# A macaron layer in split fp32 on one core: keys transposed once, decay columns in two passes, x by half pairs and in scratch during the mixer, weight terms requested ahead

## The chip, the core and the metric

The kernel runs on one core of a Trainium2 chip. The metric is device time in microseconds. Three runs of the kernel before took 1249.96, 1250.2 and 1250.56 us, the median 1250.2. One more execution was profiled; it took 1248.93 us, and its trace spans 1247.2 us. Lines named L.. are lines of the kernel file. TensorE is called PE in the trace, VectorE DVE, ScalarE ACT, GpSimdE POOL, SyncE SP. SP computes nothing here: it issues DMA requests, one behind the other.

## The reference: what is computed

One layer works on 520 tokens: a prompt of 512 and eight single tokens, each with its own states. The model width is 1024, the hidden width of an FFN 2816 = 22 x 128; all values are fp32.

```python
def layer(x, pos, s_ret, s_gdn, s_conv, ...):
    x = x + 0.5 * rmsnorm(swiglu(rmsnorm(x, ffn1_pre_g), ffn1_w_gate, ffn1_w_up, ffn1_w_down), ffn1_post_g)
    m, s_ret_new, s_gdn_new, s_conv_new = token_mixer(rmsnorm(x, mix_pre_g), ...)
    x = x + rmsnorm(m, mix_post_g)
    x = x + 0.5 * rmsnorm(swiglu(rmsnorm(x, ffn2_pre_g), ffn2_w_gate, ffn2_w_up, ffn2_w_down), ffn2_post_g)

def token_mixer(h, ...):
    proj = (h @ w_in).astype(f32)
    rq, rk, rv, rg, conv_in, gz, ga, gb, gate_r, gate_g = jnp.split(proj, idx, axis=-1)
    ...   # retention: 4 heads of 128 with rotary q, k; a short convolution over q, k, v of the gated DeltaNet
    gk = gk * lax.rsqrt(jnp.sum(gk * gk, axis=-1, keepdims=True) + EPS)
    beta = jax.nn.sigmoid(gb)
    g_gdn = -jnp.exp(gdn_a_log.astype(f32)) * jax.nn.softplus(ga + gdn_dt_bias.astype(f32))
    o_g, s_gdn_new = gated_delta_chunked(gq, gk, gv, g_gdn, beta, s_gdn.astype(f32))
    ...
    y = (jax.nn.sigmoid(gate_r) * (o_r @ w_ret_branch) + jax.nn.sigmoid(gate_g) * (o_g @ w_gdn_branch))
    y = (y @ w_out).astype(h.dtype)
```

`ga` and `gb` are four columns each of `w_in`, one for each head. These eight columns are called the decay columns here.

## The kernel before, in words

**Tiles.** x lies transposed: width on 128 partitions in eight tiles, tokens along the row, in two halves of 260. A weight column block is 128x1024 (eight pieces of 128x128, one for each piece k of the width).

**Split fp32.** A weight is split into a rounded part `whi` (a cast on ACT, L301) and a rest `wlo` (a subtraction on DVE, L302); x is split the same way into `xh` and `xl` (`xhl`, L449 on ACT and L450 on DVE). `passes` (L355) does three matmuls of 128x128 by 128x260 for each k: whi with xh (L359), whi with xl (L360), wlo with xh (L361).

**FFNs.** Hidden column pairs (gate and up) are worked on one after the other. The first three pairs of FFN1 and four of FFN2 are plain products, of two raw loads each. All later pairs take seven products instead of eight half-size ones (a Strassen scheme, `product7`, names `sv`), which work on sums of weight quarters and on sums of x quarters (`token_factors`, names ta, tb, th, tl). The weight sums s1 and s3 are made in memory: SP loads one term (L235 and L236), and POOL issues a DMA that adds the other onto it (L258). a22 is the quarter loaded alone (L237). The sums s2 and s4 are made on DVE (L315, L323). `split_seven` (L304) splits one of the seven at a time, on ACT (L319) and DVE (L320). The down projections work in the same way (names `dn`), and `post` (L508) scales by the root of the mean square and adds to x (t L540 on DVE, x L542 on POOL), and splits the new x for the next stage.

**Mixer.** Projections by `w_in` column blocks, then four retention and four DeltaNet heads (`ret_head`, `gdn_head`), the decode tokens' states, the branches and `wo`. The decay columns are the first unit, padded to 128 columns; `gate_rows` scales its rows, `gates` (L1101) transposes them and computes decays on ACT and DVE. `gdn_head` transposes keys and queries by `transposed` (four TensorE transposes of 128x128 into one bank, `tr`, L1093) for their sums of squares (four Squares on ACT, L1304), and later transposes the keys once more, scaled by DVE on the way out of PSUM (L1359, `gkd`).

**Order.** Nothing is scheduled by the compiler: each engine does its instructions in the order in which the program emits them. The program advances by ticks between groups of matmuls. At each tick, `add_sums` (L255) emits the accumulations that are due, `prefetch` (L263) emits splits ahead of use, and spawned coroutines emit their next step. `load_to` (L225) emits the loads two units ahead (RAW_BUFS = 2 raw buffers), a seven pair counting as one unit. So a raw load that waits for its buffer (the reader is `wlo`, or the last sum of a pair) holds up all requests that come behind it on SP. Split weights have nine buffers; `cost` (L260) says how many a unit takes, two for a plain one and one for one of seven. `prefetch` stops where the buffers are spent. Everything larger (x, y, hidden tiles, factors, weight terms) takes one of 68 slots of a shared pool (`slot`, L205), given out in a ring; a tile waits until the slot's last reader is done.

**x.** Loaded at the start in sixteen half-tile requests (L953, L897). During the FFNs' products the x tiles are given up and loaded again in the down projection, in FFN1 from the input, in FFN2 from a copy in DRAM that `keep` stores behind the mixer (L936). During the mixer x stays in eight slots.

## Time and profile before

| what | value |
|---|---|
| three runs: lowest, median, highest | 1249.96, 1250.2, 1250.56 us |
| profiled execution | 1248.93 us |
| its span in the trace | 1247.2 us |
| mean granted TensorE clock | 0.982 |
| busy TensorE, DVE, ACT, POOL | 96%, 72%, 46%, 22% of the span |
| bytes moved by DMA | 166.61 MB, 134 GB/s in the mean |

The stages by the trace: FFN1 to about 366 us, the mixer to about 865, FFN2 from there, of which the last 14 us are the final scaling and the stores. Times in the trace are from the span's start. Rows of instructions give start, duration, engine, line, operation, output and input names, shapes and count; the bracket gives the idle time of that engine ahead of the row and what ended it. A row with x2 or more spans several instructions. Matmuls overlap, so one lasts 0.28 us in the trace and the next begins 0.12 us behind it.

### The profile page before, as it was taken

To read this page: it belongs to the slowest core of one execution; us is meant where nothing else is said; L and a number is where in the kernel's file an instruction comes from. 1 tells how busy PE (TensorE), PEld (TensorE's weight loads), DVE (VectorE), ACT (ScalarE), POOL (GpSimd) and SP (SyncE) were. 2 spreads that over 40 slices of the span, in tenths; PEclk is the share of its full clock that TensorE was granted. 3 is DMA by queue.
4 is the path that set the end of the run, shared out by engine and by line. 5 is a ranking of instruction groups with operands and counts; after the bars stand their busy time and mean duration, and the time that the engine had idled before them with its cause. 6 is when DMAs were issued, how large, how long until landed. Compare 5 with 4: busy or idle time off the path is not lost.

```text
span 1247.2 us, 25546 instructions
## 1 busy us (share of the span) xinstructions
PE 1199.9 (96%) x9953; PEld 1187.0 (95%) x9953; DVE 904.1 (72%) x1941; ACT 570.4 (46%) x1203; POOL 279.5 (22%) x502
## 2 busy tenths in 40 slices
PE   8899999999998999999999999999989999999995
PEld 7899999999998999999999999999989999999995
DVE  8788888776557887768676666547958888866554
ACT  6555666553335564312334333334635656653330
POOL 4111111000014248545441112204111111100003
PEclk8999999999999999999999999999989999999998
DMA  5677777333353233332444554322377777532352
GB/s 178 176 178 180 182 184 184 91 94 94 94 168 90 86 103 98 98 111 71 130 140 122 188 180 154 117 86 84 115 209 178 179 177 183 146 92 66 106 165 69
DMA packets 78538, 166.61 MB, mean 134 GB/s; under 512 B 16977, under 2 KB 21937, under 8 KB 78417
## 3 DMA queue, kind: packets, MB, share of 16 engines
q1 hardware_dynamic: 66128, 140.69, 35.5%
q0 software_dynamic: 12288, 24.29, 11.3%
q8 instruction: 78, 1.28, 0.4%
q14 instruction: 44, 0.35, 0.1%
HBM read 155.24 MB, written 9.70 MB: 132 GB/s over the span
## 4 chain that ended last, share of the span: by engine, by line
PE 66%; DVE 15%; DMA 7%; ACT 6%; issue 3%; POOL 2%; SPq 1%; ACTq 0%; DVEq 0%; POOLq 0%
PE sv L359 9%; PE sv L361 8%; PE sv L360 8%; PE p L359 6%; PE p L360 5%; PE p L361 5%; PE dn L361 5%; PE dn L359 5%; PE dn L360 5%; DMA s<-gu_in 4%; DVE wlo L302 3%; DMA raw<-dn_in 2%; ACT whi L301 1%; PE br L359 1%; PE br L360 1%
## 5 line engine op out<-in xcount | busy, mean ns | idle before, releaser
L359 PE MATMUL p<-xhl,whi 128*128 128x260 f32 x784 | 233.0, 297 | 0.0
L360 PE MATMUL p<-xhl,whi 128*128 128x260 f32 x784 | 223.6, 285 | 0.0
L361 PE MATMUL p<-xhl,wlo 128*128 128x260 f32 x784 | 223.1, 285 | 0.0
L359 PE MATMUL sv<-th,w 128*128 128x260 f32 x592 | 168.2, 284 | 4.5 <-ACT u L771 4.5
L302 DVE TENSOR_TENSOR wlo<-raw,whi 128x1024 fp32r<-128x1024 f32 (+2 forms) x121 | 142.6, 1184 | 40.7 <-ACT whi L301 38.9
L361 PE MATMUL sv<-th,w 128*128 128x260 f32 x592 | 168.0, 284 | 0.0
L360 PE MATMUL sv<-tl,w 128*128 128x260 f32 x592 | 167.9, 284 | 0.0
L359 PEld LDWEIGHTS p<-xhl,whi 128*128 128x128 f32 x784 | 149.7, 191 | 0.7
L360 PEld LDWEIGHTS p<-xhl,whi 128*128 128x128 f32 x784 | 149.9, 191 | 0.1
L361 PEld LDWEIGHTS p<-xhl,wlo 128*128 128x128 f32 x784 | 149.7, 191 | 0.1
L320 DVE TENSOR_TENSOR w<-s,w 128x512 fp32r<-128x512 f32 x148 | 101.4, 688 | 55.2 <-ACT w L319 53.1
L258 POOL DMA_DIRECT2D s<-gu_in x74 | 65.0, 963 | 323.0 <-DMA s<-gu_in 178.2
L359 PE MATMUL sv<-xhl,w 128*128 128x260 f32 x444 | 126.3, 284 | 6.5 <-DVE t L751 5.9
L361 PE MATMUL dn<-hh,wlo 128*128 128x260 f32 x448 | 127.1, 284 | 1.9 <-DVE wlo L302 1.9
L301 ACT CAST whi<-raw 128x1024 fp32r<-128x1024 f32 (+2 forms) x121 | 116.5, 971 | 26.1 <-DMA raw<-dn_in 18.4
L359 PE MATMUL dn<-hh,whi 128*128 128x260 f32 x448 | 127.2, 284 | 0.1
L360 PE MATMUL dn<-hl,whi 128*128 128x260 f32 x448 | 126.6, 283 | 0.0
L361 PE MATMUL sv<-xhl,w 128*128 128x260 f32 x444 | 125.9, 283 | 0.0
L360 PE MATMUL sv<-xhl,w 128*128 128x260 f32 x444 | 125.6, 283 | 0.0
L319 ACT CAST w<-s 128x512 fp32r<-128x512 f32 x148 | 91.4, 619 | 62.8 <-DVE s L315 32.8
L359 PEld LDWEIGHTS sv<-th,w 128*128 128x128 f32 x592 | 112.3, 190 | 5.2 <-ACT u L771 4.9
L360 PEld LDWEIGHTS sv<-tl,w 128*128 128x128 f32 x592 | 112.3, 190 | 0.0
(407 smaller groups left out, 3270.0 us busy)
## 6 DMA issues: line engine op xcount, KB each, us to landing
raw<-gu_in SPq DMA_DIRECT2D x50, 512.0 KB, 4.7
raw<-win_in SPq DMA_DIRECT2D x49, 512.0 KB, 3.6
s<-gu_in SPq DMA_DIRECT2D x74, 256.0 KB, 5.5
s<-gu_in POOLq DMA_DIRECT2D x74, 256.0 KB, 4.5
raw<-dn_in SPq DMA_DIRECT2D x32, 448.0 KB, 3.4
a<-gu_in SPq DMA_DIRECT2D x37, 256.0 KB, 5.8
raw<-dn_in SPq DMA_DIRECT2D x16, 512.0 KB, 3.6
x<-x SPq DMA_DIRECT2D x16, 260.0 KB, 5.4
```

What stands on the lines that cost most here:

```text
L258: self.nc.gpsimd.dma_start(out=out, in_=term, accum_op=ALU.add)
L301: self.nc.scalar.copy(hi[:, ks], t[:, ks])
L302: self.nc.vector.tensor_tensor(lo[:, ks], t[:, ks], hi[:, ks].bitcast(F32), ALU.subtract)
L319: nc.scalar.copy(w[:, 0], t[i])
L320: nc.vector.tensor_tensor(w[:, 1], t[i], w[:, 0].bitcast(F32), ALU.subtract)
L359: mm(ps, hi[:, k, :], xh, start=first, stop=False, skip_group_check=more)
L360: mm(ps, hi[:, k, :], xl, start=False, stop=False, skip_group_check=more)
L361: mm(ps, lo[:, k, :], xh, start=False, stop=last, skip_group_check=more)
```

## The change

Five things are changed.

1. The decay columns come as their own array of eight columns for each k (`wab`, 32 KB instead of 512 KB). Their hi and lo parts lie side by side in one tile of 16 columns, so that two passes (16 columns with xh, 8 with xl) do what three did: 32 matmuls, not 48. `gates` transposes 16 rows and adds the two parts (two copies on ACT, two adds on DVE). The unit counts as one split.
2. In each of the four DeltaNet heads the keys are copied out of PSUM on ACT at the first transposition, and the second transposition is dropped. DVE scales the copy.
3. x lies in tiles of two pieces by one half. The start's sixteen requests of 130 KB become eight of 260 KB; the layouts of input and output follow.
4. x is stored to DRAM behind FFN1 (`keep`, x1) and loaded again in the mixer's down projection (`load_x`), its eight slots are given back in between.
5. The three terms of a seven pair are requested by `begin_pair`, s3 first. For the first two pairs of an FFN `token_factors` calls it at its start; each later pair's terms stand ahead of its own raw load instead of behind it.

```diff
+AB = 2 * H
...
-            out += [("win", i, 0, 8) for i in range(n)]
+            out += [("wab", 0, 0, 8)] + [("win", i, 0, 8) for i in range(1, n)]
...
+                s1, s3, a22 = self.begun.pop((u[1], m), None) or self.begin_pair(u[1], m)
                 t = self.raw.tile([P, KD, P], F32, tag="raw", name=self.name("raw"))
-                s1, s3, a22 = (self.slot(x, (P, KH, P)) for x in ("s1", "s3", "a22"))
                 nc.sync.dma_start(out=t, in_=w[2 * m])
-                nc.sync.dma_start(out=s1, in_=w[2 * m + 1, :, 0:KH])
-                nc.sync.dma_start(out=s3, in_=w[2 * m, :, 0:KH])
-                nc.sync.dma_start(out=a22, in_=w[2 * m + 1, :, KH:KD])
-
-                self.sums_due.append((self.now + SUM_LAG, self.raw_next, s1, w[2 * m + 1, :, KH:KD]))
-                self.sums_due.append((self.now + SUM_LAG, self.raw_next, s3, w[2 * m + 1, :, 0:KH]))
                 t = [t[:, 0:KH], s3, None, a22, t[:, KH:KD], s1, None]
             elif u[0] == "down7":
                 t = []
...
-                t = self.raw.tile([P, k1 - k0, P], F32, tag="raw", name=self.name("raw"))
+                t = self.raw.tile([P, k1 - k0, AB if kind == "wab" else P], F32, tag="raw", name=self.name("raw"))
...
+    def begin_pair(self, f, m):
+
+        dma, w = self.nc.sync.dma_start, self.a[f"gu{f}"]
+        s1, s3, a22 = (self.slot(x, (P, KH, P)) for x in ("s1", "s3", "a22"))
+        dma(out=s3, in_=w[2 * m, :, 0:KH])
+        dma(out=s1, in_=w[2 * m + 1, :, 0:KH])
+        dma(out=a22, in_=w[2 * m + 1, :, KH:KD])
+
+        g = self.group[self.unit_list.index(("seven", f, m, 0))]
+        self.sums_due.append((self.now + SUM_LAG, g, s3, w[2 * m + 1, :, 0:KH]))
+        self.sums_due.append((self.now + SUM_LAG, g, s1, w[2 * m + 1, :, KH:KD]))
+        return s1, s3, a22
 
...
-        return 1 if self.unit_list[j][0] in ("seven", "down7") else 2
+        return 1 if self.unit_list[j][0] in ("seven", "down7", "wab") else 2
...
+        if self.unit_list[j][0] == "wab":
+
+            self.load_to(j)
+            w, t = self.whl.tile([P, KD, 2 * AB], F32R, tag="w", name=self.name("wab")), self.loaded[self.group[j]]
+            self.split_done[j] = (w,)
+            self.started(j)
+            self.nc.scalar.copy(w[:, :, 0:AB], t)
+            self.nc.vector.tensor_tensor(w[:, :, AB:], t, w[:, :, 0:AB].bitcast(F32), ALU.subtract)
+            return
...
+        if len(w) == 1:
+            mm(ps[0 : 2 * AB], w[0][:, k, :], xh, start=first, stop=False)
+            mm(ps[0:AB], w[0][:, k, 0:AB], xl, start=False, stop=last)
+            return
...
+    def x_tiles(self):
+
+        return [[self.slot("x", (P, 2, HC)) for _ in range(KH)] for _ in range(2)]
+
+    def x_of(self, k, hf):
+        return self.x[hf][k // 2][:, k % 2]
+
...
-            self.x = [self.slot("x") for _ in range(KD)]
-            for k in range(KD):
-                nc.sync.dma_start(out=self.x[k], in_=x_from[:, k, :])
+            self.x = self.x_tiles()
+            for hf in range(2):
+                for k in range(0, KD, 2):
+                    nc.sync.dma_start(out=self.x[hf][k // 2], in_=x_from[:, hf, k : k + 2])
...
             yield 0
+
+        for m in range(PLAIN[f], PLAIN[f] + 2):
+            self.begun[f, m] = self.begin_pair(f, m)
...
         self.spawn(begin())
         xs, r = self.ffn(PLAIN[1], xs, r, V_G1PRE, self.gh[:, 0:8], V_MPRE, plus1, None, a["xT"])
-        xs, r = self.mixer(xs, r, plus2)
-        x2 = self.dram.tile([P, KD, TOK], F32, name="x2")
-
-        def keep():
-            while len(xs[1]) < KD or r[1] is None:
-                yield 0
-            for k in range(KD):
-                nc.sync.dma_start(out=x2[:, k, :], in_=self.x[k])
-                yield 1
-
-        self.spawn(keep())
+        x1, x2 = (self.dram.tile([P, 2, KD, HC], F32, name=n) for n in ("x1", "x2"))
+        self.spawn(self.keep(x1, xs, r))
+        xs, r = self.mixer(xs, r, plus2, x1)
+        self.spawn(self.keep(x2, xs, r))
         self.ffn(PLAIN[2], xs, r, V_G2PRE, self.gh[:, 8:16], None, plus2, None, x2)
         self.finish()
+
+    def keep(self, out, xs, r):
+
+        x = self.x
+        while len(xs[1]) < KD or r[1] is None:
+            yield 0
+        for hf in range(2):
+            for k in range(0, KD, 2):
+                self.nc.sync.dma_start(out=out[:, hf, k : k + 2], in_=x[hf][k // 2])
+                yield 1
     def load_first(self):
...
-            for z in (k, k + 1):
-                nc.sync.dma_start(out=self.x[z][:, 0:HC], in_=a["xT"][:, z, 0:HC])
+            nc.sync.dma_start(out=self.x[0][k // 2], in_=a["xT"][:, 0, k : k + 2])
...
         for i in range(NCH):
-            self.tr(pt[:, i * 8 : i * 8 + 8], rows[0:8, i * P : (i + 1) * P])
-        self.tr(pt[0:DEC, 32:40], rows[0:8, SEQ:TOK])
+            self.tr(pt[:, i * 16 : i * 16 + 16], rows[0:16, i * P : (i + 1) * P])
+        self.tr(pt[0:DEC, 64:80], rows[0:16, SEQ:TOK])
+        ab = c.tile([P, 5, AB], F32, name="ab")
+        nc.gpsimd.memset(ab, 0.0)
+        pl = self.small("pl", [P, 5, AB])
+        ptv = pt[:, 0:80].rearrange("p (c g) -> p c g", g=16)
+        for rs, cs in ((slice(0, P), slice(0, NCH)), (slice(0, DEC), slice(NCH, 5))):
+            nc.scalar.copy(pl[rs, cs], ptv[rs, cs, AB:])
+            nc.vector.tensor_tensor(ab[rs, cs], ptv[rs, cs, 0:AB], pl[rs, cs], ALU.add)
         ga = c.tile([P, 5, H], F32, name="ga")
         gb = c.tile([P, 5, H], F32, name="gb")
-        nc.gpsimd.memset(ga, 0.0)
-        nc.gpsimd.memset(gb, 0.0)
-        dt = self.vec[:, V_DT : V_DT + H]
-        ptv = pt[:, 0:40].rearrange("p (c g) -> p c g", g=8)
-        nc.vector.tensor_tensor(ga[:, 0:4, :], ptv[:, 0:4, 0:4], dt.unsqueeze(1).to_broadcast([P, 4, H]), ALU.add)
-        nc.vector.tensor_tensor(ga[0:DEC, 4, :], ptv[0:DEC, 4, 0:4], dt[0:DEC], ALU.add)
-        nc.vector.tensor_copy(gb[:, 0:4, :], ptv[:, 0:4, 4:8])
-        nc.vector.tensor_copy(gb[0:DEC, 4, :], ptv[0:DEC, 4, 4:8])
+        nc.vector.tensor_tensor(ga, ab[:, :, 0:H], self.vec[:, V_DT : V_DT + H].unsqueeze(1).to_broadcast([P, 5, H]), ALU.add)
         yield 8
         t = [self.small(f"sp{i}", [P, 5, H]) for i in range(5)]
...
+        kd = sl("gkd", (P, NCH, P))
         for src, off in ((k, NCH), (q, 0)):
             pt = self.transposed(src)
+            if off:
+                nc.scalar.copy(kd.rearrange("p c i -> p (c i)"), pt)
             for i in range(NCH):
...
-        kd = sl("gkd", (P, NCH, P))
-        pk = self.transposed(k)
-        nc.vector.tensor_tensor(kd, pk.rearrange("p (c i) -> p c i", i=P), self.bc(rkd), ALU.mult)
+        nc.vector.tensor_tensor(kd, kd, self.bc(rkd), ALU.mult)
```

**SP, the first seven pairs of FFN2.** Here `raw` of gu_in are the plain pairs' loads up to L251 (L246 in the change) and a seven pair's own at L234 (L235), `s` and `a` the terms, x the copies to DRAM. Before:

```order
L251 DMA raw_11552<-gu_in 128x1024
L251 DMA raw_11558<-gu_in 128x1024
L251 DMA raw_11800<-gu_in 128x1024
L251 DMA raw_11806<-gu_in 128x1024
L936 DMA x_11496<-x_4736 128x520
...
L936 DMA x_11496<-x_4739 128x520
L234 DMA raw_11918<-gu_in 128x1024
L235 DMA s_1969_11919<-gu_in 128x512
L236 DMA s_1970_11920<-gu_in 128x512
L237 DMA a_1971_11921<-gu_in 128x512
```

And in the change:

```order
L246 DMA raw_11538<-gu_in 128x1024
L246 DMA raw_11544<-gu_in 128x1024
L254 DMA s_1936_11768<-gu_in 128x512
L255 DMA s_1935_11767<-gu_in 128x512
L256 DMA a_1937_11769<-gu_in 128x512
L254 DMA s_1939_11774<-gu_in 128x512
L255 DMA s_1938_11773<-gu_in 128x512
L256 DMA a_1940_11775<-gu_in 128x512
L246 DMA raw_11798<-gu_in 128x1024
...
L975 DMA x_5035<-x_11019 128x520
L235 DMA raw_11920<-gu_in 128x1024
L975 DMA x_5035<-x_11020 128x520
```

Six terms now stand ahead of the last two plain loads; before, the first of them stood behind these, behind stores of x and behind its pair's raw.

**SP, the first seven pairs of FFN1.** Before:

```order
L251 DMA raw_284<-gu_in 128x1024
L234 DMA raw_395<-gu_in 128x1024
L235 DMA s_68_396<-gu_in 128x512
L236 DMA s_69_397<-gu_in 128x512
L237 DMA a_70_398<-gu_in 128x512
L234 DMA raw_524<-gu_in 128x1024
L235 DMA s_101_525<-gu_in 128x512
L236 DMA s_102_526<-gu_in 128x512
```

In the change:

```order
L246 DMA raw_276<-gu_in 128x1024
L254 DMA s_59_361<-gu_in 128x512
L255 DMA s_58_360<-gu_in 128x512
L256 DMA a_60_362<-gu_in 128x512
L254 DMA s_62_367<-gu_in 128x512
L255 DMA s_61_366<-gu_in 128x512
L256 DMA a_63_368<-gu_in 128x512
L235 DMA raw_399<-gu_in 128x1024
L235 DMA raw_524<-gu_in 128x1024
L254 DMA s_128_676<-gu_in 128x512
```

The six terms of two pairs stand ahead of both raws; the third pair's terms follow the second pair's raw.

**DVE, the end of FFN1.** `wlo_4829` belongs to the last down unit, the next split to the decay columns, and `wlo_4974` (`wlo_4845` in the change) to the unit behind them. Before:

```order
L302 TENSOR_TENSOR wlo_4829<-raw_4756,whi_4828 128x1024
L302 TENSOR_TENSOR wlo_4835<-raw_4808,whi_4834 128x1024
L461 TENSOR_TENSOR acc_643_3494<-acc_643_3494,s_4908 128x260
L608 TENSOR_SCALAR y_4907<-dn_4840,gh 128x260
L414 SCALAR_TENSOR_TENSOR ms_4935<-ss_4931,plus_12_135 87x3
L540 TENSOR_TENSOR t_4961<-y_3714,rb_4957 128x260
L540 TENSOR_TENSOR t_4970<-y_4007,rb_4957 128x260
L302 TENSOR_TENSOR wlo_4974<-raw_4832,whi_4973 128x1024
L540 TENSOR_TENSOR t_4993<-y_4063,rb_4957 128x260
```

In the change:

```order
L319 TENSOR_TENSOR wlo_4821<-raw_4748,whi_4820 128x1024
L308 TENSOR_TENSOR wab_4826<-raw_4800,wab_4826 128x8x8
L319 TENSOR_TENSOR wlo_4845<-raw_4824,whi_4844 128x1024
L489 TENSOR_TENSOR acc_643_3486<-acc_643_3486,s_4905 128x260
L636 TENSOR_SCALAR y_4904<-dn_4831,gh 128x260
L435 SCALAR_TENSOR_TENSOR ms_4932<-ss_4928,plus_12_127 87x3
L568 TENSOR_TENSOR t_4958<-y_3706,rb_4954 128x260
L568 TENSOR_TENSOR t_4967<-y_3999,rb_4954 128x260
L568 TENSOR_TENSOR t_4984<-y_4055,rb_4954 128x260
```

The split of the unit behind the decay columns moves from behind the first two `t` of the scaling to ahead of the last `acc`. On ACT its `whi` moves in the same way ahead of `s`, which feeds that `acc`.

More of the change, by code (lines that the diff above doesn't have):

```diff
@@ L270, in prefetch @@
             j = self.split_next
-            seven = self.cost(j) == 1
+            seven = self.unit_list[j][0] in ("seven", "down7")
             if self.unit_list[j][0] == "seven" and self.hold_sums and not force:
@@ L464, in square @@
         c0, n = HALVES[hf]
-        x, out = self.x[k][:, c0 : c0 + n], self.sq[k][:, c0 : c0 + n]
+        x, out = self.x_of(k, hf), self.sq[k][:, c0 : c0 + n]
         if eng is self.nc.scalar:
@@ L666, in first_units @@
                     if hf:
-                        self.release()
+                        self.release(len(ws[j]))
                     else:
-                        banks[j][0] = early[j // 2][:, j % 2 * HC : j % 2 * HC + cols]
-                        self.nc.scalar.copy(banks[j][0], ps[j])
+                        rows = 2 * AB if len(ws[j]) == 1 else P
+                        banks[j][0] = early[j // 2][0:rows, j % 2 * HC : j % 2 * HC + cols]
+                        self.nc.scalar.copy(banks[j][0], ps[j][0:rows])
                 if hf:
@@ L679, in token_factors @@
             yield 0
+        for m in range(PLAIN[f], PLAIN[f] + 2):
+            self.begun[f, m] = self.begin_pair(f, m)
         tt, stt = nc.vector.tensor_tensor, nc.vector.scalar_tensor_tensor
         for k in range(KH):
-            x1, x2 = self.x[k], self.x[k + KH]
-            x11, x12, x21, x22 = x1[:, 0:HC], x1[:, HC:TOK], x2[:, 0:HC], x2[:, HC:TOK]
+            x11, x12, x21, x22 = (self.x_of(z, hf) for z in (k, k + KH) for hf in range(2))
             g1, g2 = (self.vec[:, gcol + z : gcol + z + 1] for z in (k, k + KH))
@@ L885, in run @@
         nc.sync.dma_start(out=self.vec, in_=a["vec"])
-        self.x = [self.slot("x") for _ in range(KD)]
+        self.x = self.x_tiles()
         self.ones = c.tile([P, P], F32, name="ones")
@@ L1759 @@
 OUTS = {
-    "yT": (P, KD, TOK),
+    "yT": (P, 2, KD, HC),
     "sretp": (H, P, P),
```

34 lines of the change are left out of this document (17 added, 17 removed).

## Prediction

> **What bounds the kernel now.** I read the busy time of the engines first, then what TensorE waited for, then the busy time by stretch, and at last the chain of waits up to each place that stood out.
>
> ```profile
> PE 1199.9 (96%) x9953; PEld 1187.0 (95%) x9953; DVE 904.1 (72%) x1941; ACT 570.4 (46%) x1203; POOL 279.5 (22%) x502
> PE sv L359 <- DVE t L751: 5.9, 1, 5.9
> PE sv L359 <- ACT u L771: 4.5, 2, 3.8
> PE sv L359 <- DVE v L788: 0.5, 1, 0.5
> 62.00:240.00 178.00, 178.00 (x1489) 178.00 (x1488) 151.08 (x295) 107.36 (x222) 27.96 (x32) 1.00 0.69 172
> 374.00:400.00 26.00, 22.65 (x187) 21.77 (x187) 21.60 (x42) 16.57 (x38) 12.83 (x16) 1.00 0.25 69
> 432.00:640.00 208.00, 202.04 (x1751) 198.45 (x1751) 154.82 (x439) 77.62 (x182) 113.63 (x284) 0.99 0.35 105
> 912.00:923.00 11.00, 5.05 (x31) 4.88 (x30) 7.94 (x15) 5.48 (x11) 1.74 (x2) 0.69 0.68 165
> ```
>
> The rows of waits give the total, how often, and the longest. The rows of stretches give length, busy PE, PEld, DVE, ACT and POOL, then the granted clock, the DMA share and GB/s. TensorE is busy for 1199.9 of 1247.2 us (9953 matmuls, 0.12 each), so about 47 us can be won without removing a product. Two single waits, 5.9 and 3.8 us, both before `sv` products, hold a fifth of that. From 62 to 240 us the same kind of product runs with nothing idle: a pair in steady flow costs no wait, and only the first pairs of each FFN do.
>
> **Terms requested ahead, FFN1.** This is the chain up to the second seven-product pair, and TensorE and ScalarE there.
>
> ```profile
> 42.67 0.33 SPq L234
> 43.05 3.91 DMA s<-gu_in
> 48.15 7.91 DMA s<-gu_in
> 56.16 1.14 ACT L319 CAST w<-s 128x512 fp32r<-128x512 f32 x2 [5.09 <-DMA s<-gu_in]
> 53.55 0.28 PE L361 MATMUL sv<-th,w 128*128 128x260 f32 x1
> 57.62 0.39 PE L359 MATMUL sv<-th,w 128*128 128x260 f32 x1 [3.80 <-ACT u L771]
> 59.09 0.42 PE L360 MATMUL sv<-tl,w 128*128 128x260 f32 x1
> 61.86 0.42 PE L359 MATMUL sv<-th,w 128*128 128x260 f32 x1
> 62.08 0.33 PE L360 MATMUL sv<-tl,w 128*128 128x260 f32 x1
> ```
>
> The wait is put down to the copy `u`, but ScalarE holds that copy behind casts which stood 5.09 us for a sum. The sum's load left SP only at 43.05, behind a raw load that waited for a raw buffer until 42.67; then come 3.91 us of load and 7.91 us of accumulation. In the change both terms of this pair leave SP before that raw load, behind plain raws, the last of which is issued near 26 us:
>
> ```profile
> 21.22 5.43 SPq L251 DMA_DIRECT2D raw<-gu_in  x2
> 35.81 1.97 POOL L258 DMA_DIRECT2D s<-gu_in  x2 [7.71 <-DMA s<-gu_in]
> ```
>
> Six term DMAs at about 0.47 us each leave by 30; the first pair's accumulations start at 35.81 now, so the second's, behind them on POOL, start by 38 and with the slow 7.91 are in by 46. ScalarE would go on at 56.16 − 5.09 = 51.07, and `u`, which follows the two casts (1.14), at 52.2 instead of 57.3: ahead of 53.55, where TensorE's last matmul before the wait starts. So the **3.80 us** go whole. Behind the wait matmuls follow each other by 0.22 us (61.86 to 62.08) and last 0.42 where 0.28 is usual; from about 58.7 to 62.1 that is 3.4 us at 0.12/0.22 of the pace, some 1.5 us lost. I take 5.3 in all; the bounds are 2 (half of the idle time: the raw load of 42.67, which does not move, or the DVE splits end last instead) and 5.5. What is late next is the third pair: its terms now leave right behind the raw load of 42.67, ten us ahead of before.
>
> ```profile
> 431.36 0.42 PE L360 MATMUL p<-xhl,whi 128*128 128x260 f32 x1
> ```
>
> Whether the slow stretch goes with a wait that is only shortened is open. This row, slow at 431.36, stands a little behind a wait of 1.11 us and some short products (427.78, below), so by the trace a short wait may keep it. [...]
>
> **Terms requested ahead, FFN2.**
>
> ```profile
> 868.04 21.24 SPq L251 DMA_DIRECT2D raw<-gu_in  x4
> 898.91 0.43 SPq L235 DMA_DIRECT2D s<-gu_in  x1
> 905.02 8.29 DMA s<-gu_in
> 884.60 1.65 POOL L416 TENSOR_TENSOR rs<-ms,mhalf 87x6 f32<-87x6 f32 x1 [7.58 <-DVE ms L412]
> 914.03 0.69 DVE L320 TENSOR_TENSOR w<-s,w 128x512 fp32r<-128x512 f32 x1 [8.77 <-ACT w L319]
> 918.48 0.76 DVE L751 TENSOR_TENSOR t<-g,rb 128x260 f32<-128x260 f32 x2
> 912.82 0.28 PE L361 MATMUL u<-xhl,wlo 128*128 128x260 f32 x1
> 919.05 0.56 PE L359 MATMUL sv<-xhl,w 128*128 128x260 f32 x1 [5.95 <-DVE t L751]
> 922.39 0.28 PE L359 MATMUL sv<-th,w 128*128 128x260 f32 x1
> ```
>
> The wait named is on `t` (L751), which empties the PSUM bank. On DVE that `t` stands behind the splits of the first pair, which stood 8.77 us for the cast of a sum. The sum's second term left SP at 898.91 only. In the change the six terms stand on SP between the two raws issued near 869 and the two that wait until about 888. They land near 877 by the 5 us that such a load takes, POOL is free from 886.3, and four accumulations of up to 8.29, two and two, are done by 903. Then DVE goes on at 914.03 − 8.77 = 905.3. The work from there to `t` takes 918.48 − 914.03 = 4.45 us, so `t` runs at 909.8 and `u`'s last matmul at 912.82 is not held up. The **5.95 us** go, with 3.0 us of margin. From 919.05 to 922.39 TensorE was slow again (3.34 us, 1.5 lost): 7.4 together, bounds 3 (half the idle) and 7.6. Raw loads of these pairs do not come earlier: they wait for the splits of `u`. The smaller `sv` waits, 4.5 − 3.8 = 0.7 on `u` and 0.5 on `v`, follow late terms of later pairs; I take half, 0.6, bounds 0 and 1.2.
>
> **Keys transposed once.** Per head four transposes go:
>
> ```profile
> 418.43 0.60 PE L1093 MATMUL tr<-cst,cv 128*128 128x128 f32 x4
> 418.79 0.36 PE L359 MATMUL p<-xhl,whi 128*128 128x260 f32 x1
> 427.78 0.40 PE L1146 MATMUL gc<-gg,cst 128*128 128x16 f32 x2 [1.11 <-ACT s L1304]
> L1245 ACT ACTIVATE kd<-tr,kcol 128x512 f32<-128x512 f32 x4 | 2.8, 688 | 3.9 <-PE tr L1093 3.9
> ```
>
> They take 418.79 − 418.43 = 0.36 us, times four 1.4; in the heads' stretch TensorE is busy 202 of 208 us, so most of it counts: 1.2, bounds 0 and 1.8 (the matmul behind them lasts 0.36 where 0.28 is usual, 0.08 more a head). ScalarE gains a copy of 128x512 out of PSUM, by the nearest row 0.69 us. For three heads its 46% share hides that; if not, it would be 0.7 each. In the first head TensorE stands 1.11 us at `gc` for the squares, and the copy is put before them: +0.6, bounds 0 and 0.7.
>
> **Decay columns.** Of 48 matmuls 16 go, at 0.12 us 1.9 us of TensorE. They lie in the passage to the mixer, where DVE, POOL and ScalarE set the pace:
>
> ```profile
> 365.46 0.43 DVE L461 TENSOR_TENSOR acc<-acc,s 128x260 f32<-128x260 f32 x1 [0.79 <-ACT s L460]
> 365.57 1.05 ACT L301 CAST whi<-raw 128x1024 fp32r<-128x1024 f32 x1
> 371.08 1.71 DVE L302 TENSOR_TENSOR wlo<-raw,whi 128x1024 fp32r<-128x1024 f32 x1
> 366.92 0.55 PE L422 MATMUL ss<-ones,acc 128*87 128x1 f32 x6
> ```
>
> TensorE stands 3.35 of 26 us there (374 to 400), so matmuls taken away become longer waits. The unit also counts as one split instead of two, which moves the next unit's `whi` and `wlo` ahead of FFN1's last `s` and `acc`: the cast ends at 365.57 + 1.05 = 366.6, a `wlo` of 1.2 at 367.8, and `acc` behind it at 368.2 where it was 365.9. `ss` at 366.92 had 1.0 to spare, so the chain behind it (mean square, root, x) starts 1.3 later. The 1.71 us at 371.08 are given back, largely under POOL's adds. I take **+0.8**, bounds −1.9 (the matmuls count whole) and +2 (the 1.3, and one copy of `gates` at 0.7 on the chain).
>
> **x by half pairs and in scratch.** At the start SP has eight DMAs fewer, but DVE is busy 18.76 of the 20 us from 4 to 24:
>
> ```profile
> 4.00:24.00 20.00, 17.50 (x102) 15.79 (x101) 18.76 (x31) 14.39 (x36) 11.65 (x15) 0.74 0.75 225
> 790.15 20.94 SPq L251 DMA_DIRECT2D raw<-wo_in  x5
> ```
>
> So 0, bounds −1 (x there sooner) and +0.5 (the first pair lands later than the first tile did). In the mixer eight stores and eight loads of 260 KB are new, where the DMA share is 0.35. The loads stand on SP ahead of the seventh `wo` raw; eight at 0.47 us are 3.8 us of queue, while five raws there took 20.94, so the delay is about one raw's step. The raws run one to two units ahead of the products, so I take 0; the bounds are 0 and +2 (half a step comes through).
>
> **Sum** against the profiled execution (1248.93 us, span 1247.2, so 1.7 lie around the span): −5.3 −7.4 −0.6 −1.2 +0.6 +0.8 = −13.1. Span 1234.1, execution 1235.8. The median of the runs is 1250.2, 1.3 above that execution, so **1237**. All lower bounds at once give −19, all upper ones +0.2; that many at one end is unlikely, and the likeliest case's own range is 1232 to 1242.
>
> **Rivals.**
> - *Half the waits stay.* Where the casts, DVE splits or raw loads end last as soon as the sums are early, stall one gives 2 and stall two 3. For it: the raw load of 42.67 leaves as before. Against it: 3.0 us of margin in FFN2. 1237 + 3.3 + 4.4 = 1244.7. [...]
> - *TensorE time counts whole.* The 1.9 us of the decay columns and 1.8 of transposes count, nothing is added in the passage and head: 1237 − 2.7 − 0.6 − 0.6 = 1233. For it: the 96%. Against it: the 3.35 us idle in that passage.
> - *The change does not do what it says*: the terms stand on SP until slots of the shared pool come free, so their loads leave no sooner. The first pairs then keep their waits, and 1250 stays. Against it: the mixer gives eight x slots back, and the last branch work is long done by 869.
> - *Slower:* SP takes its requests in order, and with terms one raw earlier a term that waits for a slot holds up the next raw. Late in the `sv` stages (before 240 and 1095) most slots hold hidden tiles. A raw takes 4.7 us to land and a pair is split within one of 10 us, so a raw late by more than 5 us costs a wait; four pairs in each FFN late by 3 would cost 24 us and give 1261. It decides from the slot's release coming later than the raw buffer's. Against it: 178.00 of 178 us busy now.
>
> ```profile
> raw<-gu_in SPq DMA_DIRECT2D x50, 512.0 KB, 4.7
> ```
>
> **How the numbers follow.** My forecast 0.55, half the waits 0.22, whole TensorE time 0.11, no effect 0.05, slower 0.07. About 0.2% (2.5 us) is what a measurement of this kernel tells from no change. The first three cases are faster; the fourth is the same: faster 0.88, same 0.05, slower 0.07. The range reaches from 1231 to 1246, over the first three; the last two are left out.
>
> **What would show it.** Right: no wait over 1 us before `sv` in the first 62 us and near 912; the s loads of FFN2 issued near 869; clock 1.00 in 912 to 923. Right for the passage: `ss` near 367 now waits about 1.2 us, while the matmuls of the decay columns save nothing by 400. Wrong: SP standing at L254 while the next raw is due, a wait of TensorE on a split in the last pairs, or `gc` not moving with the copy.

## Result, and the profile after

The change took 1240.86 us (median of four runs, 1238.32 to 1241.69) where before took 1250.38; the ratio is 0.9913, 95% interval 0.9888 to 0.9938, so 8 to 14 us faster. The profiled execution took 1238.32 us against 1248.93, 10.6 less; the prediction had 13.1 less by its sum. By the medians the change is 9.5 us less.

The busy times and what TensorE waited for (total, times, longest), of the change:

```profile
PE 1197.2 (97%) x9921; PEld 1184.5 (96%) x9921; DVE 902.7 (73%) x1940; ACT 576.2 (47%) x1209; POOL 280.5 (23%) x501
PE ss L443 <- DVE acc L489: 4.5, 4, 1.8
PE ss L443 <- DVE sq L509: 2.9, 2, 2.5
PE cs L1568 <- DVE gsq L1680: 2.8, 1, 2.8
PE sp L1625 <- DMA sd<-sgdn_in: 1.6, 1, 1.6
PE tr L1127 <- ACT cv L1250: 1.0, 1, 1.0
```

Before:

```profile
PE ss L422 <- DVE acc L461: 3.6, 3, 1.8
PE ss L422 <- DVE sq L481: 1.9, 2, 1.4
PE cs L1532 <- DVE gsq L1644: 1.7, 1, 1.7
```

No wait before `sv` is left: 5.9, 4.5 and 0.5 us are gone from the list. In their place the waits of the passage and the mixer have grown: `ss` on `acc` from 3.6 to 4.5, `ss` on `sq` from 1.9 to 2.9, `cs` from 1.7 to 2.8, and `tr` on `cv` is new. The stretches of time, with the columns of the prediction:

```profile
0.00:62.00 62.00, 57.85 (x423) 55.86 (x424) 53.56 (x100) 38.96 (x84) 20.73 (x31) 1.00 0.70 202
374.00:400.00 26.00, 22.04 (x160) 20.73 (x158) 18.25 (x32) 12.70 (x28) 10.61 (x11) 0.87 0.22 69
432.00:640.00 208.00, 200.45 (x1721) 196.93 (x1721) 152.50 (x433) 78.47 (x184) 114.96 (x285) 0.98 0.35 105
912.00:923.00 11.00, 11.00 (x94) 11.00 (x93) 9.10 (x20) 6.95 (x16) 1.73 (x2) 1.00 0.97 219
923.00:1095.00 172.00, 172.00 (x1435) 172.00 (x1434) 143.61 (x278) 103.15 (x211) 24.61 (x28) 1.00 0.64 159
```

The seven-product stages are full now (11.00 of 11, 172.00 of 172). The heads' stretch is emptier than before (200.45 of 208, where it had 202.04).

Where the time went and came back is read best by one and the same matmul in both traces: its start in the change minus its start before. The columns behind are the experiments below, of which each has one profile.

| matmul, its start before | change | terms alone | without terms | without keys | terms and half pairs |
|---|---|---|---|---|---|
| first `ss`, 23.66 | +0.4 | −0.3 | +0.2 | +0.6 | +1.0 |
| first `dn`, 247.63 | −5.5 | −3.3 | −0.3 | −5.3 | −5.5 |
| `ss`, 366.92 | −4.3 | −3.3 | +1.0 | −3.9 | −6.1 |
| `p` behind the passage, 399.09 | −4.3 | −3.4 | +2.6 | −3.9 | −6.1 |
| `gc`, 427.78 | −3.7 | −3.4 | +3.1 | −2.6 | −6.1 |
| `cs`, 494.06 | −2.2 | −3.4 | +4.9 | −2.6 | −6.2 |
| `gbc`, 583.23 | −0.9 | −3.5 | +7.7 | −0.5 | −7.4 |
| `dn` of the mixer, 811.38 | −0.7 | −3.3 | +7.8 | −1.6 | −6.3 |
| first `dn` of FFN2, 1103.76 | −10.0 | −11.2 | +8.8 | −11.1 | −16.2 |
| last `ss`, 1232.30 | −11.3 | −12.2 | +7.6 | −12.2 | −18.0 |

The change wins 5.9 us in FFN1 (from +0.4 to −5.5), loses 4.8 from there to the end of the mixer's products, and wins 9.3 in FFN2 up to the first `dn`, and 1.3 from there to the last `ss`.

The 4.8 us are not waits alone. Between these two `dn` TensorE does 32 matmuls fewer, which at 0.12 us each saves about 4 us. It stands idle for 16.8 us instead of 12.9, and by the trace's record its granted clock is at one half for 20.5 us instead of 10.2, which costs about 5 (an estimate from the pace: products begin 0.22 us apart in such a stretch and 0.12 elsewhere). A stretch at half clock is called slow here, as in the prediction. One lies right behind a wait for a state load at `sp`; first the change, where that wait is 1.61 us, then before at the same place in its work, where it is 0.76, with the clock as the third number from the end:

```profile
556.60:560.00 3.40, 3.40 (x17) 3.40 (x18) 0.92 (x3) 0.00 (x0) 0.00 (x0) 0.50 0.08 27
```

```profile
559.00:562.40 3.40, 3.40 (x30) 3.40 (x29) 2.43 (x7) 0.00 (x0) 0.12 (x1) 1.00 0.06 22
```

Between these two `dn` the slow stretches add up to 10.2 us in each of the six profiles without the two-pass decay columns (before and five experiments), and to 13.7 to 27.3 us in the eight with them.

### The profile page after: what moved, and what is told of

The parts are those of the page before. It is cut to its first block, busy times and chain, and to the rows that moved or that the text cites. A ratio compares the mean times of both kernels' runs of the same rounds, so it can differ in the third digit from the quotient of the medians.

```text
span 1236.6 us, 25500 instructions
## 1 busy us (share of the span) xinstructions
PE 1197.2 (97%) x9921; PEld 1184.5 (96%) x9921; DVE 902.7 (73%) x1940; ACT 576.2 (47%) x1209; POOL 280.5 (23%) x501
## 4 chain that ended last, share of the span: by engine, by line
PE 73%; DVE 13%; ACT 5%; DMA 3%; issue 3%; POOL 2%; SPq 1%; DVEq 0%; ACTq 0%; POOLq 0%
PE sv L381 10%; PE sv L380 10%; PE sv L382 10%; PE p L380 5%; PE p L382 5%; PE p L381 5%; PE dn L380 5%; PE dn L382 5%; PE dn L381 5%; DVE wlo L319 3%; DVE cv L1242 2%; DMA raw<-dn_in 1%; PE br L380 1%; PE br L381 1%; PE br L382 1%
## 5 line engine op out<-in xcount | busy, mean ns | idle before, releaser
L380 PE MATMUL p<-xhl,whi 128*128 128x260 f32 x768 | 229.9, 299 | 0.0
L382 PE MATMUL p<-xhl,wlo 128*128 128x260 f32 x768 | 220.4, 287 | 0.2 <-DVE wlo L319 0.2
L381 PE MATMUL p<-xhl,whi 128*128 128x260 f32 x768 | 220.0, 286 | 0.0
L266 POOL DMA_DIRECT2D s<-gu_in x74 | 65.3, 994 | 285.6 <-DMA s<-gu_in 138.2
L382 PEld LDWEIGHTS sv<-th,w 128*128 128x128 f32 x592 | 111.7, 189 | 0.0
L380 PEld LDWEIGHTS sv<-th,w 128*128 128x128 f32 x592 | 111.4, 188 | 0.0
```

What stands on the lines that cost most here:

```text
L266: self.nc.gpsimd.dma_start(out=out, in_=term, accum_op=ALU.add)
L380: mm(ps, hi[:, k, :], xh, start=first, stop=False, skip_group_check=more)
L381: mm(ps, hi[:, k, :], xl, start=False, stop=False, skip_group_check=more)
L382: mm(ps, lo[:, k, :], xh, start=False, stop=last, skip_group_check=more)
```

## Experiments

All experiments were compared with the kernel before on their own chip, in five rounds, in three groups of four. Intervals are about 0.25% of the time, 3 us, on each side. Differences between kernels of one group below 3 us are read from traces, as lengths of stretches between the same matmuls. Each run has one profile, so a difference of one slow stretch (3.4 us at clock 0.50, about 1.7 lost by that) can be chance.

### Taking parts away

**Terms alone.** The kernel before with `begin_pair` and its calls.

```diff
+                s1, s3, a22 = self.begun.pop((u[1], m), None) or self.begin_pair(u[1], m)
...
                 nc.sync.dma_start(out=t, in_=w[2 * m])
-                nc.sync.dma_start(out=s1, in_=w[2 * m + 1, :, 0:KH])
...
+        for m in range(PLAIN[f], PLAIN[f] + 2):
+            self.begun[f, m] = self.begin_pair(f, m)
```

> The kernel before with the earlier requests of the weight terms alone (point 5 of the change); all else as before. Theory: the requests are the whole gain and the other points cost some 3 us in the passage to the mixer and in the heads. Then this kernel is 12 to 15 us faster than before (1236 to 1238), as fast as the whole change or faster, the waits of 3.8 and 5.9 us before sv are gone, and the passage and the mixer keep their old lengths. Rival: whatever is won in FFN1 is given back in the mixer by chains that wait for DMAs and for the clock, whoever wins it. Then it is at 1240 like the whole change, with longer waits at cs and sp in the mixer.

1236.58 us, ratio 0.9891 (0.9864 to 0.9918). Its waits:

```profile
PE ss L429 <- DVE acc L468: 3.6, 3, 1.8
PE cs L1542 <- DVE gsq L1654: 1.7, 1, 1.7
PE ss L429 <- DVE sq L488: 1.4, 1, 1.4
PE ss L429 <- DVE sq L930: 1.3, 1, 1.3
PE gc L1156 <- ACT s L1314: 1.1, 1, 1.1
```

Both waits before `sv` are gone, and the passage and the mixer are those of before: 3.6 on `acc`, 1.7 at `cs`, 1.1 at `gc`. In the table its column stands at −3.3 to −3.5 from 247 to 811. The gain of FFN1 is carried through the mixer whole, so the rival (the mixer takes back what anyone wins) falls: the losses belong to the other points.

**Without the terms.** The change with the requests as before.

```diff
-                s1, s3, a22 = self.begun.pop((u[1], m), None) or self.begin_pair(u[1], m)
...
                 nc.sync.dma_start(out=t, in_=w[2 * m])
+                nc.sync.dma_start(out=s1, in_=w[2 * m + 1, :, 0:KH])
...
```

> The change without point 5 (terms requested as before, behind their own raw load); the other four points stay. Theory: 1252 to 1255, slower than before by 2 to 4 us, with both waits before sv back. Rival (the other points are worth something by themselves): 1246 to 1249.

1255.79 us, ratio 1.0045 (1.0023 to 1.0068): slower than before by 3 to 9 us, more than was expected. Both `sv` waits are back:

```profile
PE sv L386 <- DVE t L787: 5.6, 1, 5.6
PE sv L386 <- ACT u L807: 4.1, 3, 3.0
```

The four other points together cost time, and the terms are more than all of the gain. The loss lies between 247 and 583 (−0.3 to +7.7 in the table). It is waits and slow stretches together: up to 811 this profile has 4.4 us more idle time than before and 27.3 us at half clock, where before has 10.2.

**Keys transposed twice.** The change without the copy, with `transposed(k)` again.

```diff
-            if off:
-                nc.scalar.copy(kd.rearrange("p c i -> p (c i)"), pt)
...
-        nc.vector.tensor_tensor(kd, kd, self.bc(rkd), ALU.mult)
+        kd = sl("gkd", (P, NCH, P))
+        pk = self.transposed(k)
+        nc.vector.tensor_tensor(kd, pk.rearrange("p (c i) -> p c i", i=P), self.bc(rkd), ALU.mult)
```

> The change with the keys transposed a second time in each head, as before, and no copy on ScalarE. Theory: the copy of about 0.7 us on ScalarE delays the convolution's work on ScalarE and DVE, while the transposes taken away lay beside waits of TensorE; then this kernel is 1 to 3 us faster than the change (1238 to 1240), the wait at tr on cv (0.98 us) is gone and the one at cs is about 1.7 us instead of 2.8. Rival: the transposes count, and it is 1 to 2 us slower than the change (1242 to 1243).

1236.61 us, ratio 0.9897 (0.9870 to 0.9923), beside 0.9907 (0.9886 to 0.9928) for the change in the next group, on another chip: no difference that can be told. The second transposition lies behind `cs`, at 518, 582, 642 and 690 us. At the first of them, this kernel and then the change (the other four transposes are of v):

```profile
517.92 1.09 PE L1127 MATMUL tr<-cst,cv 128*128 128x128 f32 x8
```

```profile
518.10 0.66 PE L1127 MATMUL tr<-cst,cv 128*128 128x128 f32 x4
```

So 0.43 us of TensorE go in each head, 1.7 in all. Ahead of `cs` the only difference is the copy on ScalarE, and it shows at `gc`; this kernel, then the change:

```profile
425.18 0.40 PE L1181 MATMUL gc<-gg,cst 128*128 128x16 f32 x2 [0.66 <-ACT s L1339]
PE cs L1567 <- DVE gsq L1679: 1.7, 1, 1.7
```

```profile
424.06 0.29 PE L1181 MATMUL gc<-gg,cst 128*128 128x16 f32 x2
491.83 0.38 PE L1568 MATMUL cs<-ones,gsq 128*64 128x1 f32 x2 [2.78 <-DVE gsq L1680]
```

With the copy `gc` waits for nothing, TensorE comes to `cs` earlier and waits there 2.8 us instead of 1.7: DVE's `gsq` comes when it comes. All profiles agree: without the copy `gc` waits 0.65 to 1.17 us and `cs` at most 1.7 (nine profiles), with it `gc` waits for nothing and `cs` 2.6 to 3.0 (five). Why the copy frees `gc` is not settled. One expectation failed: the wait of `tr` on `cv` stayed (0.99 us) without the key copy, so the copy is not its cause.

**The next unit's split at its old place.** The change with the decay columns' unit counted as two splits.

```diff
-        return 1 if self.unit_list[j][0] in ("seven", "down7", "wab") else 2
+        return 1 if self.unit_list[j][0] in ("seven", "down7") else 2
...
-                        self.release(len(ws[j]))
+                        self.release()
```

> The change with the decay columns' unit counted as two splits, as before, so that the split of the unit behind it comes behind the first two t of the scaling again; the two passes stay. Theory: the early split costs 1 to 1.5 us in the passage to the mixer; this kernel is 0.5 to 1.5 us faster than the change (1239.5 to 1240.5), and ss near 361 waits for nothing. Rival: the split only changes its place and the time stays within 0.5 us of the change.

1236.12 us, ratio 0.9888 (0.9859 to 0.9917): not told apart from the change. The wait it was to remove is gone: `ss` near 361 stands for nothing, where in the change there is

```profile
362.67 0.62 PE L443 MATMUL ss<-ones,acc 128*87 128x1 f32 x6 [1.18 <-DVE acc L489]
```

But `sp` waits 1.7 and 1.9 us, where it waits 1.6 and 1.2 in the change, and up to the mixer's `dn` the slow stretches add up to 27.3 us, where the change has 20.5. There its profile stands at −0.1, no better than the change's −0.7.

### The decay columns, the scratch and the half pairs

The second group asked what in these points costs. The trace of the change had a row that the prediction had not thought of. ScalarE and DVE, in the mixer's first convolution:

```profile
412.40 0.17 ACT L1149 COPY pl<-gt 128x32 f32<-128x32 f32 x1
415.18 0.15 ACT L1149 COPY pl<-gt 8x8 f32<-8x8 f32 x1 [2.61 <-DVE ab L1150]
415.25 1.67 ACT L1250 ACTIVATE cv<-cv 128x512 f32<-128x512 f32 x3
413.83 1.22 DVE L319 TENSOR_TENSOR wlo<-raw,whi 128x1024 fp32r<-128x1024 f32 x1
414.96 0.18 DVE L1150 TENSOR_TENSOR ab<-gt,pl 128x32 f32<-128x32 f32 x1
415.92 0.65 PE L1127 MATMUL tr<-cst,cv 128*128 128x128 f32 x4 [0.98 <-ACT cv L1250]
```

`gates` copies the large block, adds it, copies the small block, adds it. The second copy writes the tile that the first add reads, so it waits for that add, which DVE has behind a split. The convolution's three activations stand behind that 8x8 copy, and TensorE behind them.

**The change again**, for a comparison on one chip; nothing is edited.

> The change itself, so that the kernels beside it are compared with it on one chip. Theory and rival both: 9 to 12 us faster than before (1238 to 1241).

1237.46 us, ratio 0.9907 (0.9886 to 0.9928).

**Both copies ahead of both adds.**

```diff
             nc.scalar.copy(pl[rs, cs], ptv[rs, cs, AB:])
+        for rs, cs in ((slice(0, P), slice(0, NCH)), (slice(0, DEC), slice(NCH, 5))):
             nc.vector.tensor_tensor(ab[rs, cs], ptv[rs, cs, 0:AB], pl[rs, cs], ALU.add)
```

> The change, with both ScalarE copies of gates put ahead of both DVE adds. In the change the second copy (8x8) stands 2.61 us on ScalarE for the first add, which DVE has behind three convolution steps and a split; the convolution's last step on ScalarE waits behind it, and TensorE 0.98 us for that. Theory: the copies wait for nothing, the wait of tr on cv near 416 is gone, and the passage from the mixer's first convolution to gc is 1 us shorter; the whole is 0 to 1.5 us faster than the change, since the wait at cs near 492 takes back a part. Rival: ScalarE is late by its own work (the copies' time, not the wait), and the 0.98 us stay.

1236.07 us, ratio 0.9903 (0.9876 to 0.9929). The rows of ScalarE:

```profile
410.82 0.22 ACT L1149 COPY pl<-gt 128x32 f32<-128x32 f32 x2
410.95 1.15 ACT L1251 ACTIVATE cv<-cv 128x512 f32<-128x512 f32 x2
412.36 0.63 ACT L1251 ACTIVATE cv<-cv 128x512 f32<-128x512 f32 x1 [0.27 <-DVE cv L1243]
```

The copies wait for nothing, the first two activations follow at once, and no wait at `tr` near 414 is left. So the cause is the order of copy and add, and not the copies' time. From the `p` of 399.09 to `gc` this kernel needs 27.5 us, the change 29.2 and 28.5 in its two profiles: the expected 1 us or more. As with the late split, the whole time is not told apart from the change; `cs` waits 2.7.

**Without keys and scratch.** Terms, half pairs and decay columns stay.

```diff
-        self.spawn(self.keep(x1, xs, r))
-        xs, r = self.mixer(xs, r, plus2, x1)
+        xs, r = self.mixer(xs, r, plus2, None)
```

and the edit of the keys as above. (Keys transposed once with x in its slots was not run.)

> The change without the points on keys and on x in scratch (keys transposed twice, x in its slots during the mixer): terms, half pairs and decay columns stay. Theory: the stores and loads of x cost the mixer 0.5 to 1 us, seen in the wait of sp on a state load near 556 (1.42 us without the keys point, 0.80 with the terms alone), so this kernel is 0.5 to 1.5 us faster than the change without the keys point (1235 to 1236). Rival: the wait at sp comes from the decay columns or the clock, and stays at 1.4 us; the time stays at 1236 to 1237.

1236.14 us, ratio 0.9901 (0.9876 to 0.9926), the same as without the keys alone (0.9897, on another chip). The wait at `sp` near 553 is 2.0 us, longer and not shorter, so the rival is right: the scratch costs nothing that can be told.

**Terms and half pairs.** As above, and the decay columns as before.

```diff
-            out += [("wab", 0, 0, 8)] + [("win", i, 0, 8) for i in range(1, n)]
+            out += [("win", i, 0, 8) for i in range(n)]
...
```

> Terms ahead and x by half pairs alone; decay columns, keys and x in the mixer as before. Theory: the decay columns are what makes the mixer longer; this kernel has the mixer of before (no wait at tr on cv, 1.1 us at gc, 0.8 at sp), and is at 1235 to 1237, like the terms alone. Rival: the half pairs cost or give something of their own at the start, where the first sum of squares stands 0.4 to 1.1 us later than with the terms alone: 1237 to 1238.

1233.52 us, ratio 0.9875 (0.9851 to 0.9899), the fastest of its group: all six runs (1230.1 to 1235.37) lie below all six of the change (1235.97 to 1238.73). Its waits in the passage and the mixer are those of before, as expected:

```profile
PE ss L443 <- DVE acc L489: 3.6, 3, 1.8
PE ss L443 <- DVE sq L509: 1.7, 2, 1.5
PE cs L1565 <- DVE gsq L1677: 1.7, 1, 1.7
PE gc L1179 <- ACT s L1337: 1.1, 1, 1.1
PE sp L1622 <- DMA sd<-sgdn_in: 1.0, 1, 1.0
```

This kernel and the one before it differ by the decay columns alone, 0.9875 to 0.9901. Their intervals overlap, but the traces say the same: at `gc` −6.1 us against −4.3 without keys and scratch, at the mixer's `dn` −6.3 against −1.4. The state load `sd` is waited for 1.3 to 2.2 us at `sp` near 553 in every profile with the two-pass decay columns, and 0.8 to 1.0 in every one without them. Right behind that wait lies a slow stretch of 3.4 us in all eight profiles with them, and in one of the six without. SP issues that load behind twelve small requests of the matrix inverse, and why those come later is not settled.

### The third group

> Terms ahead and x by half pairs, once more, beside the terms alone on one chip. Theory: the half pairs bring the first sum of squares' wait and a slow stretch near 27 us down and are worth 1 to 3 us in all, so 1233 to 1235. Rival: the difference of the first comparison was the clock, and both kernels are within 1 us of each other.

> The terms ahead alone, once more. Theory: 1235 to 1237, 1 to 3 us slower than with the half pairs, with 1.3 us of wait at the first ss. Rival: the same as with the half pairs within 1 us.

Terms and half pairs: 1232.69 us, ratio 0.9859 (0.9826 to 0.9892). Terms alone: 1238.4 us, ratio 0.9899 (0.9875 to 0.9923). By the first two groups the half pairs are 2 us better (0.9891 to 0.9875, on two chips), by this one 5 (0.9899 to 0.9859, whose intervals overlap at the edge). The first `ss` waits 1.1 and 1.3 us for DVE with the terms alone, and for nothing in the two profiles with half pairs; in the next kernel, which has the half pairs too, it waits 1.05. That wait is no gain: the product that waits starts at 25.1 to 25.3 us in all these profiles and in before, and with half pairs TensorE only comes there later. A gain that repeats lies late in the `sv` stages: from the 401st `sv` product of an FFN to its first `dn` the terms alone need 143.9 us in FFN1 and 133.9 in FFN2, with half pairs 143.3 and 133.2, in both profiles of each. Most of the rest between these profiles is slow stretches: near 27 us in one of the two with the terms alone, and near 860 for 6.8 us in both of them, against 3.4 us and none. So the gain is likely; some 1 us of it is placed, and its full size and its cause are open.

**Terms ahead for the first two pairs only.** Terms and half pairs, with each later pair's terms behind its own raw load.

```diff
-                s1, s3, a22 = self.begun.pop((u[1], m), None) or self.begin_pair(u[1], m)
                 t = self.raw.tile([P, KD, P], F32, tag="raw", name=self.name("raw"))
                 nc.sync.dma_start(out=t, in_=w[2 * m])
+                s1, s3, a22 = self.begun.pop((u[1], m), None) or self.begin_pair(u[1], m)
```

> Half pairs of x and terms ahead, but ahead only for the first two pairs of each FFN; each later pair's terms stand behind its own raw load again. Theory: the two large waits stay gone, the small waits before sv in FFN2 (0.70 and 0.53 us before) come back, and perhaps the wait moves from the second pair to the third; 1 to 4 us slower than terms ahead for all (1235 to 1238). Rival: the first two pairs are all of the gain, and the time is the same within 1 us.

1235.48 us, ratio 0.9871 (0.9846 to 0.9895), against 0.9859 with the terms of all pairs ahead. Only one small wait before `sv` came back (0.42 us), and FFN2 needs 134.5 us from the 401st `sv` to the first `dn`, 1.3 more. So the first two pairs are nearly all of the gain, though the whole times are not told apart.

**Terms, half pairs and repaired decay columns.** The decay columns in two passes, with the late split and both copies first.

> Terms ahead, half pairs, and the decay columns in two passes with the next unit's split where it stood before and both copies of gates ahead of both adds. Theory: the two repairs take away what the decay columns cost (1.2 us at ss, 1.0 at tr), and the 1.9 us of products taken away turn into waits at ss near 390 and cs near 490; the same as without the decay columns, within 1 us (1233 to 1235). Rival: the two passes count, and it is 1.5 to 2 us faster (1231 to 1232); or the waits at sp near 553 stay long, and it is 2 us slower.

1236.39 us, ratio 0.9880 (0.9851 to 0.9910): not better than without them, and nearest to the last of its expectations. In the waits

```profile
PE ss L443 <- DVE acc L489: 3.9, 3, 1.8
PE ss L443 <- DVE sq L509: 2.9, 2, 2.4
PE sp L1624 <- DMA sd<-sret_in: 2.2, 1, 2.2
PE sp L1624 <- DMA sd<-sgdn_in: 1.5, 1, 1.5
```

the longest wait of `ss` on `sq` is 2.4 us, without the decay columns 1.5 and 1.4, and the two waits for states at `sp` are 1.5 and 2.2, where the two profiles of terms and half pairs have 1.0 and 1.2, and 0.9 and none. From `cs` to the mixer's `dn` it needs 320.0 us, those two 317.2 and 316.8. In the passage the products taken away became waits, and nothing was gained even with the repairs. The version that beats both kernels is terms with half pairs, at 0.9859 and 0.9875.

## Why the prediction was right, and where its steps failed

The time lay inside the range and the sign was right; the sum was 2.5 us too good by the profiled executions and 3.6 by the medians, and it hides two errors of opposite sign, the decay columns (dearer than forecast) and the half pairs (likely worth more). That these cancel in part is luck. The two stalls were sized rightly.

**Terms, FFN1: right.** The third row is of ScalarE, where 51.07 was forecast:

```profile
26.81 0.42 SPq L254 DMA_DIRECT2D s<-gu_in  x1
33.33 1.75 POOL L266 DMA_DIRECT2D s<-gu_in  x2 [0.19 <-issue]
51.08 1.14 ACT L336 CAST w<-s 128x512 fp32r<-128x512 f32 x2
```

−5.3 was forecast. From the first `sv` product to the 401st, which holds the wait and the slow stretch behind it, before needs 53.7 us, the change 47.9 and the terms alone 48.1 in both profiles: −5.7 and −5.6. The granted clock of the first 62 us went to 1.00; before it was 0.89:

```profile
0.00:62.00 62.00, 53.66 (x376) 51.37 (x377) 48.60 (x89) 36.21 (x78) 19.26 (x29) 0.89 0.64 177
```

**Terms, FFN2: right, and the small waits under-sized.** The loads were forecast near 869, the first cast's rest at 905.3 and `t` at 909.8, in a kernel that was 0.7 us ahead by then:

```profile
868.93 0.77 SPq L254 DMA_DIRECT2D s<-gu_in  x1
904.55 0.68 DVE L337 TENSOR_TENSOR w<-s,w 128x512 fp32r<-128x512 f32 x1
908.99 0.76 DVE L783 TENSOR_TENSOR t<-g,rb 128x260 f32<-128x260 f32 x2
```

The stall and its slow stretch are gone whole: from the first `u` of FFN2 to its 401st `sv` before needs 72.9 us, the change 65.3 and the terms alone 65.5, −7.6 and −7.4 where −7.4 was forecast. From there to the first `dn` it is −1.7 in the change and −1.3 with the terms alone, for the later pairs, where −0.6 was forecast with −1.2 as the bound.

**Keys: the step that failed** is "in the heads' stretch TensorE is busy 202 of 208 us, so most of it counts". That share is an average, and two of the four transpositions lie behind that stretch. The transposes do go, 1.7 us in all, near the bound of 1.8. But from `cs` to the mixer's `dn` the change needs 318.9 and 320.7 us in its two profiles, and 318.3 without the keys point: TensorE still meets `po` and `sp` there, where POOL or a DMA ends last, and has 10.2 us at half clock where the other has 6.8. The forecast of +0.6 at the first head failed the other way: with the copy `gc` no longer waits at all, and what is won there is waited away at `cs`. In the whole time the point is not told apart from 0 (0.9897 to 0.9907), within the bounds of 0 to −1.8.

**Decay columns: the mechanism in the passage was right, the size of the whole was not.** The early split put `ss` 1.18 us behind `acc` (1.3 forecast), and the products taken away turned into wait: `ss` on `sq` stands

```profile
393.06 1.18 PE L443 MATMUL ss<-ones,sq 128*87 128x1 f32 x7 [2.45 <-DVE sq L509]
```

where it stood 1.41, and from the `ss` of 366.92 to the `p` of 399.09 before and the change need 32.2 us (the change's second profile 31.5). Two things were missed. One is the order of copy and add in `gates`: the term had copies at 0.7 us as its upper bound, and no wait of a copy for an add of DVE. The other comes 140 us later and stood in no term: the longer wait for the state load at `sp` near 555 and the slow stretch behind it. +0.8 was forecast, 2.6 us is what the pair of experiments gives (0.9901 to 0.9875, with overlapping intervals), outside the upper bound of +2. The two repairs did not win it back in any whole time: they mend the passage, and the loss at `sp` stays. Why that load comes later is open.

**Half pairs: the step that failed** is the term of 0 with the bound of −1. Its reason, that DVE is busy at the start, holds there: the `ss` that waits for DVE starts at 25.1 to 25.3 us with half pairs and without. The two comparisons nevertheless give 2 and 5 us. Some 1 us lies late in the `sv` stages, which the term did not look at; the rest goes with slow stretches in these profiles, and whether the half pairs cause them is not settled.

**Scratch: right.** Nothing that can be told.

The rivals: *half the waits stay* and *no effect* fell with the rows of `sv`. *TensorE time counts whole* fell: the passage is at most 0.7 us shorter in the change for its 16 matmuls less, and the keys show no gain in the whole time. *Slower* fell: TensorE is busy in all of the 172 us up to 1095, the place where a late raw would have shown. The loss that did come was in the mixer, for which the prediction had only the scratch as a candidate.

## What to carry to other kernels

A gain at a wait that is traced back to a late request can be sized to a fraction of a microsecond from the chain. It shows best between two matmuls close around it: there the profiles with the terms ahead agree within 0.3 us, while whole times move by 2 to 3. A gain in busy time of the busiest engine can't be sized so, since an engine that is 97% busy still stands at the few points where others end last. For work taken from such an engine, look for the next place where it waits for another engine, and expect the gain to end there, as it did here with the decay columns' 16 products (`ss` waits 2.45 us on `sq` instead of 1.41). And when an instruction is put between others of an engine, ask for each of its operands when that will be ready: an 8x8 copy of 0.15 us held ScalarE for 2.61 us.

## What was not expected of the hardware

The slow stretches of TensorE come behind waits as short as 1.11 us, and not behind every longer one. In before they begin 1.0 to 3.0 us behind the ends of waits of 1.41 (`ss`, 398.14), 1.11 (`gc`, 427.78), 1.74 (`cs`, 494.06) and 1.80 us (`ss`, 863.29), and none begins behind one of 1.60 us (`po`, 545.37). Near 620 us all kernels but one have a wait for a state load at `sp`, followed by eight products of one column (about 1 us) and then full products. In the profiles with a wait of 0.56 to 0.87 us (three kernels) the products behind are at full pace. Between 1.24 and 1.65 us (five) they are slow in three and not in two: before has 1.27 us without a slow stretch, the change 1.24 with one. From 1.87 to 2.53 (five) they are slow in all. Two of the thirteen, in which a product of 0.42 us is a slow one; first the change, then terms ahead for the first pairs only, where no slow product follows:

```profile
620.49 1.02 PE L1625 MATMUL sp<-rdec,sd 128*128 128x1 f32 x8 [1.24 <-DMA sd<-sret_in]
621.69 0.42 PE L381 MATMUL p<-xhl,whi 128*128 128x260 f32 x1
```

```profile
616.84 1.02 PE L1622 MATMUL sp<-rdec,sd 128*128 128x1 f32 x8 [0.69 <-DMA sd<-sret_in]
```

By the record of the granted clock such a stretch lasts 3.41 us in before and the change (ten of them) or 6.83 us (two, which begin while TensorE still waits), the start and the end of the trace left aside. Where TensorE is busy in it, it costs about half its length, by the 17 products of the change in 3.40 us where before has 30. That is as much as several of the effects studied here, and the length of the wait alone does not fix whether it comes. It is a part of the 3 us between runs of one kernel: over the 117 executions of the experiments and of before beside them, a lower mean clock goes with a longer time within each kernel (correlation −0.6), which is about a third of the variance; the rest is open.
